# Layer two's stream in a new order: memory attention first, six state updates behind the output projection

## The chip, the core and the metric

The kernel runs on one core of one Trainium2 chip. The metric is the device time of one execution in microseconds. The engines are named as in the profile: PE multiplies matrices (PEld is its loading of weights), DVE and ACT work on vectors, POOL and SP are used here almost only to issue transfers. Each engine executes its own instructions in a fixed order; semaphores make it wait for others.

## The reference, cut to what matters

One step of a two-layer decoder trunk, for 256 prompt tokens and 8 sample tokens at once (264 columns in all), width 2048. Layer one mixes tokens by sliding-window attention, layer two by a gated linear recurrence; both have four memory cross-attention heads beside it. The change is in layer two:

```python
q, f, iv, mq, g = split(h @ w_in)             # one projection of 2048 to 12*128 (q, f, v), 512 (mq), 2048 (g)
fg = lb + (1 - lb) * sigmoid(f)               # 12 heads of 128; k = 1 - fg
# prompt: chunked recurrence per head; sample: one step from a given state (8 tokens x 12 heads x 128x128)
state = fg[..., None] * state + k[..., None] * v        # hgrn_state_sample, an output
o = einsum('bhk,bhkv->bhv', silu(q), state)
o = o * rsqrt(mean(o * o) + eps) * norm_w
mem_o = softmax(mq @ mk.T * 128 ** -0.5) @ mv           # 4 heads, 256 memory rows; caches for the sample tokens
branch = concat([o, mem_o]) * silu(g)
h = layer_norm(alpha * h + branch @ w_out)
```

## The kernel before

Tokens lie in the free axis: an activation is 128 features x 264 columns, sixteen such chunks make the width. A weight tile of 2048 x 128 (1 MB) is one *unit* of a stream (`Stream`). SP loads it into `raw` (four buffers); `prep` splits it into two halves of 16 bits, the high one on ACT (L97), the low one on DVE (L98), into `hl` (four buffers); then the unit's function runs `proj`: 16 chunks times three matmuls (high-high, low-high, high-low) of 128x264 into a PSUM bank `pj`, of which there are two. What becomes of the bank depends on the unit: `f_unit` makes gate and key (`fg`, `qk32`, `kk`), `hv_unit` copies values (`hvt` with one buffer, `vs`), to be transposed on PE as `hvp` and `hvr`, `hq_unit` makes the query `hqs`, gate units make silu (`sil`), `out_unit` adds to the residual `xres`.

Work that isn't a projection stands in generators beside the stream; after each unit `pump` takes one step of the first. `hg_side` is the recurrence of a pair of heads, ten steps: products level by level (`hd`, `hs_1` to `hs_64`, in two banks `sc`), then `pk` (transposed keys, copied to `kn`), `pu` (the chunk's state, copied to `s`), `hpo` (output, copied to `osb`), squares into `osq`, `rms` (their sum over features), and on ACT `Ln` and `Exp` for the root, each behind a table load; the last DVE operation (L1189) writes `mix` for the gate. `memp_side` and the `ck` and `cv` units are memory attention for prompt and sample tokens.

`state_unit` runs per head: it loads a state of 512 KB as a unit, multiplies it by the query (`hos`), and updates it in place, block by block for eight tokens: a matmul `vb` that spreads a value row, a scaling on ACT (L1237) and a multiply-add on DVE (L1238), and writes it out on POOL's queue (`out_ss`).

Layer two's order in the stream is by pairs: f, f, v, v, then q, state and (for heads 0 to 7) gate of each head; then four memory queries; then eight cache tiles, with the late gates dealt between them; then sixteen output tiles. A tile scheduler decides, from the order in which the code issues and its own estimates, the order of instructions on each engine; it is fixed when the program is built.

Of the kernel before, what the change touches and what calls it, by code (L numbers as in the profile page):

```python
# [18 lines left out]
P = 128  # L19
NC = 16  # L20
# [13 lines left out]
NG1 = 8  # L34
# [12 lines left out]
LEVELS = (1, 2, 4, 8, 16, 32, 64)  # L47
NMASK = (len(LEVELS) - 1) * 64
# [9 lines left out]
class Stream:  # L58


    def __init__(self, nc, pool, nraw, nsplit):
        self.nc, self.pool = nc, pool
        self.nraw, self.nsplit = nraw, nsplit
        self.units = []
        self.raw = {}
        self.hl = {}

# [37 lines left out]
    def run(self, pump):  # L105
        n = len(self.units)
        loaded = prepped = 0
        free = 0

        def loads():  # L110
            nonlocal loaded
            while loaded < n and loaded < free + self.nraw:
                self.load(loaded)
                loaded += 1

        loads()
        for i in range(n):
            while prepped < min(loaded, i + self.nsplit):
                self.prep(prepped)
                if self.units[prepped][5] and free == prepped:  # L120
                    free += 1
                prepped += 1
                loads()
            self.units[i][1](self.hl.pop(i))
            del self.raw[i]
            while free < prepped and (free <= i or self.units[free][5]):
# [8 lines left out]
def trunk_kernel(  # L135
# [75 lines left out]
    bias_s = pm.tile([P, 2, NQ], F32, name="bias_s")  # L211

# [503 lines left out]

    fin = {0: deque(), 1: deque()}
# [14 lines left out]
    def silu2(out, pt):  # L732
        nc.scalar.activation(out, pt, AF.Tanh, scale=0.5 * CP)
        nc.vector.scalar_tensor_tensor(out, out, 1.0, pt, op0=ALU.add, op1=ALU.mult)
# [10 lines left out]
    def residual(l, i, cols, n, pt):  # L745
        z = xres[:, i, cols]
        summed = nc.vector.scalar_tensor_tensor(z, z, ALPHA / CP, pt, op0=ALU.mult, op1=ALU.add)  # L747
# [235 lines left out]
    def f_unit(h):  # L983
        def fn(hl):
# [6 lines left out]
            if i == 0:  # L991
                cur["fg"] = p1.tile([P, 2, T], F32, tag="fg", name=f"fg{h}", bufs=2)
                cur["qk"] = p1.tile([P, 2, 2, TP], F32, tag="qk32", name=f"qk32_{h}", bufs=2)
                cur["kk"] = p1.tile([P, 2, TS], F32, tag="kk", name=f"kk{h}", bufs=2)
                cur["ks8"] = p1.tile([P, 2, TS], F32, tag="ks8", name=f"ks8{h}", bufs=2)
            fg, kk, ks8 = cur["fg"][:, i], cur["kk"][:, i], cur["ks8"][:, i]
# [6 lines left out]
            nc.vector.tensor_scalar_mul(ks8, kk, 1.0 / (SA * SK))  # L1003
# [5 lines left out]
    def hq_unit(h):  # L1009
        def fn(hl):  # L1010
# [5 lines left out]
            if h % 2 == 1:  # L1016
                side.append(hg_side(h // 2, cur["q"], cur["vn"], cur["fg"], cur["qk"]))
# [3 lines left out]
    later, due = [], []  # L1021

    def hv_unit(h):
        def fn(hl):
# [3 lines left out]
            if i == 0:  # L1028
                cur["vn"] = p1.tile([P, 2, 2, P], F32, tag="vn", name=f"vn{h}", bufs=2)
                cur["vr"] = p1.tile([P, 2, P], F16, tag="vr", name=f"vr{h}", bufs=2)  # L1030
# [10 lines left out]
    def hv_rows(h, vt, vs, vn, vr):  # L1041
# [7 lines left out]
        nc.vector.tensor_copy(vr[:, i], p16)  # L1049
# [14 lines left out]
    def hg_side(pi, q, vn, fg, qk):  # L1064
# [119 lines left out]
        for i, sq in enumerate(sqs):  # L1184
# [3 lines left out]
            scaled = mix[:, h] if h >= NG1 else sq  # L1188
# [3 lines left out]
            if h < NG1:  # L1192
# [4 lines left out]
    def state_unit(h):  # L1197
        def fn(hl):
            p1 = H["p"]
            pi, i = h // 2, h % 2  # L1200
            raw = stream.raw[state_at[h]][:, : TS * P]
            R = raw.rearrange("p (b v) -> p b v", b=TS)
            v = hl[:, :, : TS * P].rearrange("p s (b v) -> p s b v", b=TS)
            vr, fgs, ks8 = cur["vr"][:, i], cur["fg"][:, i, TP:T], cur["ks8"][:, i]
            qs, vts = (cur[n][:, i, TP:T] for n in ("q", "vt"))
            ks = cur["kk"][:, i]
            if i == 0:
                osb[pi] = p1.tile([P, 2, T], F32, tag="osb", name=f"osb{pi}", bufs=2)
            qk = p1.tile([P, TS], F32, tag="qk", name=f"qk{h}", bufs=2)
            qf = p1.tile([P, TS], F32, tag="qf", name=f"qf{h}", bufs=2)  # L1210
            qfh = p1.tile([P, TS, 2], F16, tag="qfh", name=f"qfh{h}", bufs=2)
            nc.vector.scalar_tensor_tensor(qf, qs, SA * 0.5 * CP, fgs, op0=ALU.mult, op1=ALU.mult)
            nc.vector.scalar_tensor_tensor(qk, qs, 8.0 * 0.5 * CP / SK, ks, op0=ALU.mult, op1=ALU.mult)
            qkh = p1.tile([P, 2, TS], F16, tag="qkh", name=f"qkh{h}", bufs=2)
            nc.scalar.activation(qkh[:, 0], qk, AF.Copy)
            nc.vector.tensor_tensor(qkh[:, 1], qk, qkh[:, 0], op=ALU.subtract)
            nc.scalar.activation(qfh[:, :, 0], qf, AF.Copy)
            nc.vector.tensor_tensor(qfh[:, :, 1], qf, qfh[:, :, 0], op=ALU.subtract)
            po = bank("ms", 1, f"hos{h}")
            pov = po[:, : 2 * TS].rearrange("p (b s) -> p b s", s=2)  # L1220
            for b in range(TS):
                mm(pov[:, b], v[:, 0, b], qfh[:, b], start=True, stop=False)
                mm(pov[:, b, 0:1], v[:, 1, b], qfh[:, b, 0:1], start=False, stop=True)
            pq = po[:, 2 * TS : 3 * TS]
            for s in range(2):
                mm(pq, H["ones"], qkh[:, s], start=s == 0, stop=s == 1)
            nc.vector.tensor_reduce(qf, pov, axis=AX.X, op=ALU.add)
            nc.vector.tensor_tensor(qk, pq, vts, op=ALU.mult)
            nc.vector.scalar_tensor_tensor(osb[pi][:, i, TP:T], qf, 1.0 / (SA * SA), qk, op0=ALU.mult, op1=ALU.add)
            for g in range(2):  # L1230
                pvb = bank("pt", 2, f"vb{h}{g}")
                for bb in range(4):
                    mm(pvb[:, bb * P : (bb + 1) * P], H["sel"][:, 4 * g + bb], vr, start=True, stop=True)
                for bb in range(4):
                    b = 4 * g + bb
                    s = R[:, b]
                    nc.scalar.activation(s, s, AF.Copy, scale=fgs[:, b : b + 1])  # L1237
                    nc.vector.scalar_tensor_tensor(  # L1238
                        s, pvb[:, bb * P : (bb + 1) * P], ks8[:, b : b + 1], s, op0=ALU.mult, op1=ALU.add
                    )  # L1240
            nc.gpsimd.dma_start(ss_o[pi, :, i * TS * P : (i + 1) * TS * P], raw)
# [3 lines left out]
    state_at = {}  # L1245
    for pi in range(HD // 2):
        for part, unit in (("f", f_unit), ("v", hv_unit)):
            for i in range(2):
                stream.add(wb(w_in1, NB1[part] + 2 * pi + i), unit(2 * pi + i))
        for h in (2 * pi, 2 * pi + 1):  # L1250
            stream.add(wb(w_in1, NB1["q"] + h), hq_unit(h))
            state_at[h] = len(stream.units)
            stream.add(state[pi][:, (h % 2) * TS * P : (h % 2 + 1) * TS * P], state_unit(h), SA, whole=True)
            if h < NG1:
                stream.add(wb(w_in1, NB1["g"] + h), early_gate(h))
    for h in range(NM):
        stream.add(wb(w_in1, NB1["mq"] + h), mq_unit(h))
# [4 lines left out]
    u = stream.units[-1]  # L1262
    stream.units[-1] = (u[0], mem1_sides(u[1]), *u[2:])

    def g1(j):
        stream.add(wb(w_in1, NB1["g"] + j), gate_unit(1, j))

    late = deque(range(NG1, NC))
    for n, (c, unit, t) in enumerate([(c_mk, ck_unit, t) for t in range(4)] + [(c_mv, cv_unit, t) for t in range(4)]):
        stream.add(c[1, t], unit(1, t), SA)  # L1270
        if late and (late[0] < NQ or n == 7 or late[0] < NQ + 2 and n > 3):
            g1(late.popleft())
    while late:
        g1(late.popleft())
    for i in range(NC):
        stream.add(wb(w_o[1], i), out_unit(1, i), home=hold if i >= NC - NSPLIT else None)

    def after(i):
# [8 lines left out]
        pump(1)  # L1287
# [23 lines left out]
def _constants():  # L1311
# [17 lines left out]
    for b in range(TS):  # L1329
        sel[b, b] = 1  # L1330
        sel[TS + b, b] = 1
# [101 lines left out]
```

## Time and profile before

| | |
|---|---|
| time, median of 3 runs | 906.81 us (906.51 to 907.01) |
| profiled execution | 906.08 us, its span 904.3 us |
| mean granted clock of TensorE | 0.994 of full |
| PE, DVE, ACT, POOL busy | 98%, 78%, 64%, 4% |
| read and written in HBM | 180 MB and 17 MB, 218 GB/s |

Layer two begins at about 430 us of the span; the last pair's chain and the memory attention are at 760 to 800, the output projection from there to about 880. Busy times are sums over an engine; the windows that the prediction shows give them for a stretch, with the granted clock (PEclk) beside.

### The profile page before, as it was taken

To read this page: it belongs to the slowest core of one execution; us is meant where nothing else is said; L and a number is where in the kernel's file an instruction comes from. 1 tells how busy PE (TensorE), PEld (TensorE's weight loads), DVE (VectorE), ACT (ScalarE), POOL (GpSimd) and SP (SyncE) were. 2 spreads that over 40 slices of the span, in tenths; PEclk is the share of its full clock that TensorE was granted. 3 is DMA by queue.
4 is the path that set the end of the run, shared out by engine and by line. 5 is a ranking of instruction groups with operands and counts; after the bars stand their busy time and mean duration, and the time that the engine had idled before them with its cause. 6 is when DMAs were issued, how large, how long until landed. Compare 5 with 4: busy or idle time off the path is not lost.

```text
span 904.3 us, 21814 instructions
## 1 busy us (share of the span) xinstructions
PE 886.6 (98%) x9281; PEld 762.9 (84%) x9281; DVE 701.5 (78%) x1230; ACT 582.4 (64%) x982; POOL 34.9 (4%) x68
## 2 busy tenths in 40 slices
PE   9999999999999999999999999999999999799996
PEld 6888889678888888876888888898888888688996
DVE  6879877669886666697687887979788989678736
ACT  6767776657664444476766877777777585858415
POOL 1100010000000000002000000000000000000000
PEclk9999999999999999999999999999999999899999
DMA  9998566557785555556374655827454878456303
GB/s 340 392 353 317 188 245 209 188 208 265 262 333 192 187 192 203 207 198 214 127 292 137 216 201 174 299 101 260 160 215 164 303 283 308 172 207 244 130 2 97
DMA packets 37853, 198.67 MB, mean 220 GB/s; under 512 B 4555, under 2 KB 10732, under 8 KB 17532
## 3 DMA queue, kind: packets, MB, share of 16 engines
q1 hardware_dynamic: 33024, 181.55, 56.3%
q0 software_dynamic: 4688, 15.67, 4.6%
q8 instruction: 72, 1.18, 0.5%
q14 instruction: 25, 0.20, 0.1%
q10 hardware_dynamic: 44, 0.07, 0.0%
HBM read 180.03 MB, written 17.22 MB: 218 GB/s over the span
## 4 chain that ended last, share of the span: by engine, by line
PE 77%; DVE 8%; ACT 6%; DMA 6%; issue 3%; SPq 0%; ACTq 0%; DVEq 0%
PE o L303 5%; PE o L305 5%; PE o L304 5%; PE g L305 5%; PE g L303 5%; PE g L304 5%; DVE hl L98 4%; ACT hl L97 2%; PE hv L305 2%; PE hv L303 2%; PE hv L304 2%; DMA raw<-in_w_in 2%; PE hq L303 2%; PE hq L305 2%; PE hq L304 2%
## 5 line engine op out<-in xcount | busy, mean ns | idle before, releaser
L98 DVE SCALAR_TENSOR_TENSOR hl<-raw,hl 128x2048 f16<-128x2048 f32 (+2 forms) x168 | 358.6, 2138 | 82.0 <-ACT hl L97 81.0
L97 ACT ACTIVATE hl<-raw 128x2048 f16<-128x2048 f32 (+2 forms) x168 | 299.2, 1784 | 97.8 <-PE o L305 45.4
L305 PEld LDWEIGHTS <-hl 128*128 128x128 f16 (+2 forms) x2048 | 197.4, 98 | 31.8 <-DVE hl L98 2.9
L303 PEld LDWEIGHTS <-hl 128*128 128x128 f16 (+2 forms) x2048 | 197.3, 98 | 30.6 <-issue 2.2
L304 PEld LDWEIGHTS <-hl 128*128 128x128 f16 (+2 forms) x2048 | 197.4, 98 | 30.3 <-issue 2.2
L305 PE MATMUL g<-xhl,hl 128*128 128x264 f16 x512 | 142.0, 277 | 2.4 <-DVE hl L98 2.4
L303 PE MATMUL g<-xhl,hl 128*128 128x264 f16 x512 | 141.9, 277 | 0.0
L304 PE MATMUL g<-xhl,hl 128*128 128x264 f16 x512 | 141.9, 277 | 0.0
L303 PE MATMUL o<-mix,hl 128*128 128x264 f16 x384 | 105.4, 276 | 0.8 <-DVE xres L747 0.8
L304 PE MATMUL o<-mix,hl 128*128 128x264 f16 x384 | 105.8, 276 | 0.0
L305 PE MATMUL o<-mix,hl 128*128 128x264 f16 x384 | 105.7, 276 | 0.0
L303 PE MATMUL q<-xhl,hl 128*128 128x264 f16 x192 | 53.0, 276 | 1.0 <-DVE kst L251 1.0
L303 PE MATMUL f<-xhl,hl 128*128 128x264 f16 x192 | 52.9, 276 | 0.4 <-DVE mvhl L251 0.4
L305 PE MATMUL hv<-xhl,hl 128*128 128x264 f16 x192 | 53.0, 276 | 0.0
L303 PE MATMUL hq<-xhl,hl 128*128 128x264 f16 x192 | 53.0, 276 | 0.0
L304 PE MATMUL hq<-xhl,hl 128*128 128x264 f16 x192 | 53.0, 276 | 0.0
L305 PE MATMUL hq<-xhl,hl 128*128 128x264 f16 x192 | 53.0, 276 | 0.0
L304 PE MATMUL hv<-xhl,hl 128*128 128x264 f16 x192 | 53.0, 276 | 0.0
L303 PE MATMUL hv<-xhl,hl 128*128 128x264 f16 x192 | 53.0, 276 | 0.0
L304 PE MATMUL q<-xhl,hl 128*128 128x264 f16 x192 | 53.0, 276 | 0.0
L305 PE MATMUL q<-xhl,hl 128*128 128x264 f16 x192 | 53.0, 276 | 0.0
L304 PE MATMUL f<-xhl,hl 128*128 128x264 f16 x192 | 52.9, 276 | 0.0
(338 smaller groups left out, 1858.4 us busy)
## 6 DMA issues: line engine op xcount, KB each, us to landing
raw<-in_w_in SPq DMA_DIRECT2D x88, 1024.0 KB, 6.4
raw<-in_w_o SPq DMA_DIRECT2D x32, 1024.0 KB, 5.0
raw<-in_w_mk SPq DMA_DIRECT2D x8, 1024.0 KB, 4.9
raw<-in_w_mv SPq DMA_DIRECT2D x8, 1024.0 KB, 4.9
raw<-in_c_mk SPq DMA_DIRECT2D x8, 1024.0 KB, 5.1
raw<-in_c_mv SPq DMA_DIRECT2D x8, 1024.0 KB, 7.0
raw<-in_state SPq DMA_DIRECT2D x12, 512.0 KB, 5.4
out_ss<-raw POOLq DMA_DIRECT2D x12, 512.0 KB, 5.5
```

The lines of the kernel that those rows point to most:

```text
L97: hi = self.nc.scalar.activation(hl[:, 0, s], raw[:, s], AF.Copy, scale=scale)
L98: lo = self.nc.vector.scalar_tensor_tensor(hl[:, 1, s], raw[:, s], scale, hl[:, 0, s], op0=ALU.mult, op1=ALU.subtract)
L303: mm(out, lhs(0), rhs(0), start=start, stop=False)
L304: mm(out, lhs(0), rhs(1), start=False, stop=False)
L305: return mm(out, lhs(1), rhs(0), start=False, stop=stop)
```

## The change

Layer two's stream is put together anew. Memory queries and cache tiles come first, dealt between the first pair's f, v, q and the gates of heads 0 and 1. A table `pumps` says how many pair steps follow each unit (0, 1 or 2). States are loaded per pair as one tile of 1 MB, and `state_unit` works per pair. Heads 0, 1, 2, 4, 6 have an early gate (a gate unit that stands ahead of the head's result); the others' gates follow the last pair, heads 10 and 11 at the end.

For heads 6 to 11 the update of the state is put off. Their value rows, gates and keys are copied (`kept`, 80 KB a pair) to HBM by POOL's queue and read back into `late_kept`; the state is fetched a second time, into the memory of `mkhl`, `mvhl` and `mqhl`, which memory attention no longer needs; and the update is issued in output units 1, 3, 5, 7, 9 and 11, on DVE behind the residual of that tile. `issue_after` binds instructions to the one named only on the engine that issued it, which here is DVE.

```diff
-NG1 = 8
+EARLY = (0, 1, 2, 4, 6)
+LATER = tuple(range(6, HD))
...
-            scaled = mix[:, h] if h >= NG1 else sq
+            scaled = sq if h in EARLY else mix[:, h]
...
+    def update(h, R, vr, fgs, ks, sel):
+        for g in range(2):
+            pvb = bank("pt", 2, f"vb{h}{g}")
+            for bb in range(4):
+                mm(pvb[:, bb * P : (bb + 1) * P], sel[:, 4 * g + bb], vr, start=True, stop=True)
+            for bb in range(4):
+                b = 4 * g + bb
+                s = R[:, b]
+                nc.scalar.activation(s, s, AF.Copy, scale=fgs[:, b : b + 1])
+                nc.vector.scalar_tensor_tensor(
+                    s, pvb[:, bb * P : (bb + 1) * P], ks[:, b : b + 1], s, op0=ALU.mult, op1=ALU.add
+                )
+        nc.gpsimd.dma_start(ss_o[h // 2, :, h % 2 * TS * P : (h % 2 + 1) * TS * P], R.rearrange("p b v -> p (b v)"))
...
+    def fetch(h):
+        if not homes:
+            aside["sel"] = cp.tile([P, TS, P], F16, tag="ms", name="late_sel", bufs=2)
+            nc.gpsimd.dma_start(aside["sel"], sel_d)
+            aside["kept"] = cp.tile([P, len(LATER), KEPT], F32, tag="ms", name="late_kept", bufs=2)
+            for pi in sorted(kept):
+                k = 2 * pi - LATER[0]
+                nc.gpsimd.dma_start(aside["kept"][:, k : k + 2], kept[pi])
...
+        nc.gpsimd.dma_start(aside[h], state[h // 2][:, (h % 2) * TS * P : (h % 2 + 1) * TS * P])
...
+    def with_update(fn, k):
+        def f(hl):
+            fn(hl)
+            with tc.issue_after(marks["o"].ins):
+                late_update(LATER[k])
+                if k + 3 < len(LATER):
+                    fetch(LATER[k + 3])
...
+            if 2 * pi in LATER:
+                tail = vr[:, :, P // 2 :]
+                nc.vector.tensor_copy(tail[:, :, :TS], fgs)
+                nc.vector.tensor_copy(tail[:, :, TS:], ks)
+                nc.gpsimd.dma_start(kept[pi], vr)
+                return
...
+    f_of(0)
+    for h in range(NM):
+        w1("mq", h, mem1_sides(mq_unit(h)) if h == NM - 1 else mq_unit(h))
+    cache(c_mk, ck_unit, 0)
+    f_of(1, 2)
+    cache(c_mk, ck_unit, 1)
+    v_of(0, 2)
...
+    for pi in range(2, HD // 2):
+        gated = 2 * pi - 2 in EARLY
+        f_of(2 * pi, 2)
+        f_of(2 * pi + 1, 1 if gated else 2)
+        v_of(2 * pi, 2)
+        v_of(2 * pi + 1, 2)
+        q_of(2 * pi)
+        q_of(2 * pi + 1)
+        state_of(pi)
+        if 2 * pi in EARLY:
+            gate_of(2 * pi)
+    last = (HD - 2, HD - 1)
...
+    for k, j in enumerate([j for j in range(NC) if j not in EARLY and j not in last] + list(last)):
+        w1("g", j, fetch_first(gate_unit(1, j)) if k == 6 else gate_unit(1, j))
     for i in range(NC):
-        stream.add(wb(w_o[1], i), out_unit(1, i), home=hold if i >= NC - NSPLIT else None)
+        unit = out_unit(1, i)
+        if i % 2 == 1 and i // 2 < len(LATER):
+            unit = with_update(unit, i // 2)
+        stream.add(wb(w_o[1], i), unit, home=hold if i >= NC - NSPLIT else None)
...
-        pump(1)
+        pump(pumps.get(i, 1))
```

The first place is the chain of pair 3 (heads 6 and 7) on PE. In the kernel before, the matmuls of that chain stand between those of the projections `hq`:

```order
L1152 MATMUL pk_9001<-ident,qk_6_7952 128x128 x4
...
L305 MATMUL hq_9018<-xhl,hl_8779 128x264
L1158 MATMUL pu_9070<-vn_8108,kn_9006 128x128 x4
L1169 MATMUL hpo_9155<-st_8506,vn_8108 128x128
L1170 MATMUL hpo_9155<-st_8506,vn_8108 128x128
L1045 MATMUL hvp_9081<-ident,hvt_8897 128x128 x2
...
L304 MATMUL hq_9170<-xhl,hl_8932 128x264
L1171 MATMUL hpo_9155<-qk_6_7952,s_9075 128x128
L1169 MATMUL hpo_9155<-st_8506,vn_8108 128x128
L1048 LDWEIGHTS vs_5660
L1048 MATMUL hvr_9085<-ident_68,vs_5660 128x128
L1170 MATMUL hpo_9155<-st_8506,vn_8108 128x128
```

Between the rows shown are 24 and 10 projection matmuls from `pk` to `pu`, and 29 from `pu` to the second `hpo`. In the changed kernel the same chain stands on PE like this, between the projections `hv` of head 11 and `hq` of head 10:

```order
L1156 MATMUL pk_9303<-ident,qk_6_8440 128x128 x4
L1173 MATMUL hpo_9378<-st_8877,vn_8599 128x128
L1174 MATMUL hpo_9378<-st_8877,vn_8599 128x128
L1162 MATMUL pu_9367<-vn_8599,kn_9308 128x128 x4
L1049 MATMUL hvp_9390<-ident,hvt_9254 128x128 x2
L1175 MATMUL hpo_9378<-qk_6_8440,s_9372 128x128
L1173 MATMUL hpo_9378<-st_8877,vn_8599 128x128
L1174 MATMUL hpo_9378<-st_8877,vn_8599 128x128
L1175 MATMUL hpo_9378<-qk_6_8440,s_9372 128x128
L1052 LDWEIGHTS vs_5662
L1052 MATMUL hvr_9394<-ident_68,vs_5662 128x128
L1049 MATMUL hvp_9467<-ident,hvt_9254 128x128 x2
```

Two rows on, `hvr` of the other head and the first matmul of `hq` follow: no projection matmul is left between the steps.

The second place is ACT in the same stretch of the changed kernel. `hvt` and `vs` are head 10's and 11's, `osq` are pair 3's squares, then `Ln` (L1187) and `Exp` (L1190); L1209 are the eight scalings of the put-off state of head 8, which the code issues in output unit 5:

```order
L1038 ACTIVATE hvt_9851<-hv_9800 128x264
L253 ACTIVATE vs_5662<-hv_9800 128x8
L1038 ACTIVATE hvt_9851<-hv_9912 128x264
L1181 ACTIVATE osq_9386<-osb_8899 128x264
L1181 ACTIVATE osq_9388<-osb_8899 128x264
L253 ACTIVATE vs_5663<-hv_9912 128x8
L1209 ACTIVATE mqhl<-mqhl,late_kept 128x128 x8
L1187 ACT_TABLE_LOAD
L1187 ACTIVATE osq_9386<-rms_9454,eps_rms 128x264
L1187 ACTIVATE osq_9388<-rms_9457,eps_rms 128x264
L1190 ACT_TABLE_LOAD
L1190 ACTIVATE osq_9386<-osq_9386 128x264
```

In the kernel before, the scalings (there L1237) of a head stand in its own state unit; head 8's have moved here, between squares and `Ln` of pair 3, and those of heads 6 and 7 stand in the same way around the `Ln` of pair 2.

The third place is the chain of the last pair (heads 10 and 11) on PE. Before, it stands behind a late gate and ahead of the sample tokens' memory attention (`mrow`, `mback`, `mso`):

```order
L1152 MATMUL pk_10521<-ident,qk_10_9379 128x128 x4
L1169 MATMUL hpo_10636<-st_10088,vn_9535 128x128
L1170 MATMUL hpo_10636<-st_10088,vn_9535 128x128
L1158 MATMUL pu_10565<-vn_9535,kn_10526 128x128 x4
L666 MATMUL mrow_10687<-ident,mst_10685 32x128 x2
L1171 MATMUL hpo_10636<-qk_10_9379,s_10570 128x128
L1169 MATMUL hpo_10636<-st_10088,vn_9535 128x128
L1170 MATMUL hpo_10636<-st_10088,vn_9535 128x128
L1171 MATMUL hpo_10636<-qk_10_9379,s_10570 128x128
L677 MATMUL mback_10698<-ident,mrows_10690 128x32 x2
L1182 MATMUL rms_10704<-osq_10644,ones_rms 128x264
L1182 MATMUL rms_10707<-osq_10646,ones_rms 128x264
```

In the changed kernel it stands ahead of the rest of the first two output tiles (`o`), and the put-off `vb` matmuls of head 6 stand between its steps:

```order
L1156 MATMUL pk_10667<-ident,qk_10_9659 128x128 x4
L1173 MATMUL hpo_10814<-st_10124,vn_9849 128x128
L1174 MATMUL hpo_10814<-st_10124,vn_9849 128x128
L1162 MATMUL pu_10743<-vn_9849,kn_10672 128x128 x4
L1205 LDWEIGHTS late_sel
L1205 MATMUL vb_11141<-late_kept,late_sel 128x128
...
L1175 MATMUL hpo_10814<-qk_10_9659,s_10748 128x128
L1173 MATMUL hpo_10814<-st_10124,vn_9849 128x128
L1174 MATMUL hpo_10814<-st_10124,vn_9849 128x128
L1175 MATMUL hpo_10814<-qk_10_9659,s_10748 128x128
...
L1186 MATMUL rms_10886<-osq_10822,ones_rms 128x264
...
L307 MATMUL o_0_11029<-mix,hl_10826 128x264
```

Memory attention is gone from there; the output projection's first tiles follow the chain's `rms`, with the low halves and the last chunks of `mix` still to come.

More of the change, by code (lines that the diff above doesn't have):

```diff
@@ L125, in run @@
             del self.raw[i]
-            while free < prepped and (free <= i or self.units[free][5]):
+            while free < prepped and (free + self.longer.get(free, 0) <= i or self.units[free][5]):
                 free += 1
@@ L211, in trunk_kernel @@
     bias_s = pm.tile([P, 2, NQ], F32, name="bias_s")
+    kept = {pi: dp.tile([P, 2, KEPT], F32, name=f"kept{pi}") for pi in sorted({h // 2 for h in LATER})}
     def small_work():
@@ L1198, in fn @@
         def fn(hl):
             p1 = H["p"]
[L1200 to L1208, printed above, removed]
@@ L1215, in fn @@
[L1215 to L1223, printed above, removed]
@@ L1224, in fn @@
-            pq = po[:, 2 * TS : 3 * TS]
+            qkh = p1.tile([P, 2, 2, TS], F16, tag="qkh", name=f"qkh{pi}", bufs=2)
+            split_from(qfh[:, :, :, 0], qfh[:, :, :, 1], qf, 1.0)
+            split_from(qkh[:, 0], qkh[:, 1], qk, 1.0)
+            po = bank("ms", 1, f"hos{pi}")
+            pov = po[:, : 4 * TS].rearrange("p (i b s) -> p i b s", i=2, s=2)
+            for i in range(2):
+                for b in range(TS):
+                    mm(pov[:, i, b], v[:, 0, i, b], qfh[:, i, b], start=True, stop=False)
+                    mm(pov[:, i, b, 0:1], v[:, 1, i, b], qfh[:, i, b, 0:1], start=False, stop=True)
@@ L1225, in fn @@
+            pq = po[:, 4 * TS : 6 * TS]
             for s in range(2):
-                mm(pq, H["ones"], qkh[:, s], start=s == 0, stop=s == 1)
+                mm(pq, H["ones"], qkh[:, s].rearrange("p i b -> p (i b)"), start=s == 0, stop=s == 1)
             nc.vector.tensor_reduce(qf, pov, axis=AX.X, op=ALU.add)
[L1228 to L1240, printed above, removed]
@@ L1241, in fn @@
-            nc.gpsimd.dma_start(ss_o[pi, :, i * TS * P : (i + 1) * TS * P], raw)
-        return fn
[L1245 to L1255, printed above, removed]
@@ new lines, in fn, with half, w1, state_of @@
+            R = raw.rearrange("p (i b v) -> p i b v", i=2, b=TS)
+            def half(i):
+                update(2 * pi + i, R[:, i], vr[:, i, : P // 2].bitcast(F16), fgs[:, i], ks[:, i], H["sel"])
+            half(0)
+            later.append(lambda: half(1))
+        return fn
+    state_at, pumps = {}, {}
+    def w1(part, i, fn, n=1):
+        pumps[len(stream.units)] = n
+        stream.add(wb(w_in1, NB1[part] + i), fn)
+    def state_of(pi):
+        at = state_at[pi] = len(stream.units)
+        pumps[at] = 0
+        whole = 2 * pi not in LATER
+        if whole:
+            stream.longer[at] = 1
+        stream.add(state[pi], state_unit(pi), SA, whole=whole)
@@ L1259, in mem1_sides, with gate_of, cache @@
+    def gate_of(h, n=1):
+        w1("g", h, early_gate(h) if h in EARLY else gate_unit(1, h), n)
+    def cache(c, unit, t):
+        pumps[len(stream.units)] = 0
+        stream.add(c[1, t], unit(1, t), SA)
     def mem1_sides(fn):
         return with_side(fn, [lambda h=h: memp_side(1, h) for h in range(NM)])
[L1262 to L1274, printed above, removed]
+    def f_of(h, n=1):
+        w1("f", h, f_unit(h), n)
+    def v_of(h, n=1):
+        w1("v", h, hv_unit(h), n)
+    def q_of(h, n=1):
+        w1("q", h, hq_unit(h), n)
+    f_of(0)
@@ new lines, in trunk_kernel, with fetch_first, f @@
+    v_of(3, 2)
+    q_of(2)
+    q_of(3)
+    state_of(1)
+    gate_of(2)
+    for pi in range(2, HD // 2):
[10 more added lines that the diff above has]
+    last = (HD - 2, HD - 1)
+    def fetch_first(fn):
+        def f(hl):
+            fn(hl)
+            with tc.issue_after(marks["silu"].ins):
+                for h in LATER[:3]:
+                    fetch(h)
+        return f
@@ L1329, in _constants @@
     for b in range(TS):
[L1330 to L1331 removed]
+        sel[b, b] = 1 / (SA * SK)
+        sel[TS + b, b] = 1 / (SA * SK)
     c["sel"] = sel
```

66 lines of the change are left out of this document (50 added, 16 removed).

## The prediction

> **What bounds the kernel now.** I read the page's first part, then layer two in stretches of 20 us and, where PE falls short, of 5 us.
>
> ```profile
> span 904.3 us, 21814 instructions
> PE 886.6 (98%) x9281; PEld 762.9 (84%) x9281; DVE 701.5 (78%) x1230; ACT 582.4 (64%) x982; POOL 34.9 (4%) x68
> ```
> ```profile
> core 0: us, PE busy (x) PEld busy (x) DVE busy (x) ACT busy (x) POOL busy (x), PEclk, DMA share, GB/s
> 740.00:760.00 20.00, 20.00 (x248) 17.69 (x247) 20.00 (x23) 14.40 (x14) 0.00 (x0) 1.00 0.91 327
> 760.00:780.00 20.00, 16.23 (x184) 13.44 (x182) 13.03 (x20) 11.82 (x19) 0.54 (x1) 0.95 0.66 240
> 780.00:800.00 20.00, 18.27 (x211) 15.25 (x210) 19.67 (x34) 15.73 (x30) 0.00 (x0) 0.88 0.58 220
> 800.00:820.00 20.00, 19.70 (x176) 17.12 (x175) 12.37 (x19) 12.12 (x18) 0.00 (x0) 1.00 0.30 103
> 820.00:840.00 20.00, 20.00 (x180) 17.39 (x178) 17.94 (x19) 14.23 (x11) 0.00 (x0) 1.00 0.92 339
> 840.00:860.00 20.00, 19.52 (x231) 18.49 (x230) 14.78 (x22) 7.83 (x9) 0.00 (x0) 1.00 0.20 79
> ```
>
> PE is the bound: 98% of the span. Layer two loses time almost only at 760 to 800, where the last head pair's chain meets the memory attention: 3.77+1.73 = 5.5 us idle, and a granted clock of 0.95 and 0.88, worth (0.05+0.12) x 20 = 3.4 us. The rows 800 and 840 add 0.30+0.48 = 0.8. So 9.7 us is what a perfect layer two would win. Busy time hides a little more, since matmuls follow each other faster than one lasts (0.11 against 0.28 us, first rows below), 0.17 us in each gap; with a dozen gaps 12 us is the most. I take 10.5.
>
> What an uncovered pair chain looks like is in the timeline of that stretch:
>
> ```profile
> 767.16 0.28 PE L305 MATMUL g<-xhl,hl 128*128 128x264 f16 x1
> 767.27 0.28 PE L303 MATMUL g<-xhl,hl 128*128 128x264 f16 x1
> ...
> 769.24 1.91 ACT L97 ACTIVATE hl<-raw 128x2048 f16<-128x2048 f32 x1 [3.84 <-issue]
> 769.31 0.63 PE L1152 MATMUL pk<-ident,qk 128*128 128x128 f32 x4
> 771.06 0.36 ACT L1147 ACTIVATE st<-hs 64x256 f32<-64x256 f32 x1
> 771.32 0.58 ACT L1154 ACTIVATE kn<-pk 128x512 f32<-128x512 f32 x1
> 772.02 1.09 PE L1158 MATMUL pu<-vn,kn 128*128 128x128 f32 x8
> 773.15 0.38 ACT L1162 ACTIVATE s<-pu 128x256 f32<-128x256 f32 x1 [1.25 <-PE pu L1158]
> 774.93 0.57 ACT L1173 ACTIVATE osb<-hpo 128x512 f32<-128x512 f32 x1
> 775.53 0.73 ACT L1177 ACTIVATE osq<-osb 128x264 f32<-128x264 f32 x2
> 776.41 1.28 ACT L1183 ACT_TABLE_LOAD   x1
> 777.71 0.85 ACT L1183 ACTIVATE osq<-rms,eps_rms 128x264 f32<-128x264 f32 x2
> 778.58 1.28 ACT L1186 ACT_TABLE_LOAD   x1
> 779.87 0.73 ACT L1186 ACTIVATE osq<-osq 128x264 f32<-128x264 f32 x2
> ...
> 780.33 0.90 DVE L1189 SCALAR_TENSOR_TENSOR mix<-osb,small_t,osq 128x264 f32<-128x264 f32 x2 [3.67 <-ACT osq L1186]
> ```
> ```profile
> 770.00:775.00 5.00, 3.02 (x22) 2.53 (x22) 3.19 (x5) 2.81 (x7) 0.40 (x1) 1.00 0.39 120
> 775.00:780.00 5.00, 3.90 (x54) 3.08 (x55) 0.72 (x3) 4.91 (x10) 0.15 (x1) 0.81 0.56 220
> 780.00:785.00 5.00, 3.71 (x95) 3.10 (x93) 4.67 (x8) 5.00 (x7) 0.00 (x0) 0.84 0.01 3
> 785.00:790.00 5.00, 4.57 (x28) 3.46 (x29) 5.00 (x7) 5.00 (x9) 0.00 (x0) 0.66 0.67 236
> 790.00:795.00 5.00, 5.00 (x46) 4.25 (x45) 5.00 (x11) 2.09 (x6) 0.00 (x0) 1.00 0.98 400
> ```
>
> In program order `pk`, `hpo`, `pu`, `hpo`, `rms` of this pair stand one behind the other on PE; the other pairs of before mostly have 10 to 50 projection matmuls between them and loses next to nothing (row 740, PE 20.00 of 20). From the start of `pu` to the end of `mix` the chain takes 781.23-772.02 = 9.2 us, and after it the granted clock is down: (0.19+0.16+0.34) x 5 = 3.4 us over three rows.
>
> **The change, part by part.** PE loses 12 `pq` matmuls of eight columns, DVE the `ks8` products and half of the state unit's eight-column operations; DVE is busy 78%, so that lies beside PE and is worth nothing. POOL's queue gets three writes and three reads of the kept rows, a second load of `sel` and six state loads, at 4% busy; only the reads have someone waiting (place A and B). SP's queue is moved past fewer, larger loads: a state tile now waits for the write of an older one, three to four projection units (16 us or more) ahead of use, against 12 us for the write and the load (6 each, rows below); hidden, and 0 to 2 us if the units run short.
>
> *Memory attention first.* Before's junction goes, as does what little stands around it: -10.5 (-9.7 to -12). The stages that now open layer two are projections interleaved with memory steps, and PE has two units of 48 matmuls between a step and its use; I take 0, and 0 to 2 for its bound.
>
> What is late next is read from where PE has nothing to do in the new order. There are three such places. They are priced with these groups and queues of layer two, and with a row of its timeline in which eight state scalings stand together:
>
> ```profile
> 691.86 2.45 ACT L1237 ACTIVATE raw<-raw,fg 128x128 f32<-128x128 f32 x8 [0.50 <-DVE hl L98]
> ```
> ```profile
> L1001 ACT ACTIVATE qk<-th,hl_lb 128x256 f32<-128x256 f32 x4 | 2.4, 588 | 0.0
> L1046 ACT ACTIVATE vn<-hvp 128x256 f32<-128x256 f32 x6 | 2.3, 376 | 0.0
> L1034 ACT ACTIVATE hvt<-hv 128x264 f32<-128x264 f32 x4 | 1.5, 384 | 3.5 <-PE hv L305 3.5
> L249 ACT ACTIVATE vs<-hv 128x8 f16<-128x8 f32 x4 | 0.7, 168 | 0.0
> L728 DVE SCALAR_TENSOR_TENSOR sil<-sil,mix 128x264 f32<-128x264 f32 x8 | 3.4, 430 | 2.0 <-ACT mix L634 1.9
> L729 ACT ACTIVATE mix<-sil 128x264 f16<-128x264 f32 x8 | 3.4, 420 | 4.7 <-DVE sil L728 4.7
> L1238 DVE SCALAR_TENSOR_TENSOR raw<-vb,ks,raw 128x128 f32<-128x128 f32 x48 | 13.4, 345 | 0.0
> ```
> ```profile
> out_ss<-raw POOLq DMA_DIRECT2D x6, 512.0 KB, 6.1
> raw<-in_state SPq DMA_DIRECT2D x4, 512.0 KB, 6.2
> ...
> out_sp<-s POOLq DMA_DIRECT2D x6, 128.0 KB, 3.1
> ```
>
> *Place A, pair 2's chain between `hv9` and `hq8`.* `hq8` takes the PSUM bank of `hv8`, so its first matmul waits until `hvt` and `vs` of head 8 are copied. `hvt` has one buffer and is free only after `hvp` of head 7, which the new order puts behind all of `hv9` and pair 2's `hpo`. From there ACT has the rest of a weight split, `osb` 0.57, two `qk32` of 0.588, `vn` 0.376, `hvt` 0.384, `vs` 0.168, and DVE one more `vs` (0.16): 2.8 us and up to 1.9 for the split, less some 0.6 of `hvr` and `hvp` on PE: 2.2 to 4.1, I take 3.4. Then eight scalings of head 6's put-off state (L1209, was L1237; 2.45) stand on ACT between the squares and `Ln`, six of head 7's between the two `Ln`s (1.8) and two behind (0.6), and they wait for `late_kept`, which was written to HBM and is read back: 2 x 3.1 = 6.2 us by the 128 KB row, of which I put 3 behind the moment at which ACT arrives (0 to 6.2). From the squares to the tanh of `hq8` ACT then needs 0.7+2.45+1.3+0.4+1.8+0.4+0.6+1.3+0.4+0.4 = 9.8 us plus that wait, 12.8; PE has `hq8` and `hq9`, 96 matmuls of 0.112 = 10.8, and 0.7 of small ones until `f10` needs the bank: 11.5. So 1.3 shows (0 to 4.5, for a whole round trip). Place A: 4.7 (2.2 to 8.6).
>
> *Place B, pair 3's chain between `hv11` and `hq10`.* Here all of the chain stands between two projections: `st` 0.36, `kn` 0.58, `pu` 1.09, `s` 0.38, `hpo` 0.6, `osb` 0.57, two `qk32` 1.18, `vn` 0.38, `hvt` 0.38, `vs` 0.17+0.16: 5.9 us, in which PE has 1.3 of its own: 4.6 (3.5, if the `qk32` go first, to 5.9). Then the same scalings for head 8, waiting for their own round trip, stand between the squares and `Ln`. `hd` and `hs` of pair 4 wait for that `Ln` (they take its PSUM banks): squares, scalings, table load and `Ln` 0.7+2.45+1.3+0.85 = 5.3, against 5.4 of `hq10` as cover, so nothing, or 3 with the same 3 us of the round trip; half-way 1.5 (0 to 4.5). Place B: 6.1.
>
> *Place C, pair 5's chain between the last gates and the output projection.* `hs_64`, `pk`, `hpo`, `pu`, `hpo`, `rms` are adjacent again, as in before's junction, and memory attention is no longer there to fill even a part. The third output tile needs a third bank and the first two need the last `mix`. `st`+`kn` 0.9, 9.2 from `pu` to `mix`, then gate, cast and low half 0.43+0.42+0.43: 11.4, less 4.1 of PE's own (`pk` 0.6, `pu` 1.1, `hpo`, `rms` and eight `vb` an estimated 2.4): 7.3 (6.5 to 8).
>
> *Clock.* Before's rows show the clock falling behind 5 us windows in which PE did 3.0 to 3.9 of work as recorded; it cost 3.4 there. I take 3 for all three places (0 to 6). The Trainium skill (TensorE: Matmul & The Clock Gate, "Part 1: The HAM clock gate") says that one idle window of about 3.4 us puts TensorE at half rate until about 3.4 us were busy; the 0.81, 0.84 and 0.66 agree with it. By that rule each place would pay 3.4 x 0.5 = 1.7 us for each window that falls idle, 5 in all.
>
> *Updates put off.* Six heads' 8 DVE updates, 8 scalings and 8 `vb` matmuls move behind the output tiles 1, 3, 5, 7, 9, 11. Before, DVE is at 17.94 of 20 in 820:840; six updates of 8 x 0.345 = 2.8 us push it over what a 5.4 us unit leaves, and the fetch of head 9 comes only after head 6's write (6.1+6.2 us on POOL's queue), with ACT waiting in order. PE has weights in hand for two units: 1 (0 to 3). The tail after 860 is unchanged.
>
> Sum: -10.5+4.7+6.1+7.3+3+1 = +11.6; span 915.9. The profiled execution was 906.08, 1.8 beside its span, and 0.7 below the median of 906.81: **918.4 us**. Its own range is 909 to 929: the small ends together give a span of 904.3-12+2.2+3.5+6.5+0+0 = 904.5, the great ones 904.3-9.7+8.6+10.4+8+6+3 = 930.6; neither comes whole. A measurement tells about 0.2% (1.8 us) from no change.
>
> **The rivals.** *The places are filled (faster, 0.2).* If ACT and DVE run so far ahead of PE that `hvt`, `st` and `kn` are done when PE arrives, A and B cost nothing and only C is left, partly (3): 904.3-10.5+3 = 896.8, and 2.5 beside the span: 899 us, 896 to 904. For it: ACT and DVE are busy 64% and 78%. Against: every wait in A and B starts from a PE result of the same chain, which no early start of another engine shortens. It decides when A, B and C together are below 10.5.
>
> *Only the chains cost, the round trips are hidden (slower or the same, 0.17; of it 0.07 within 0.2%).* The kept rows land before ACT arrives: A 3.4, B 4.6, C 6.5 and a clock of 1.5 give 904.3-10.5+16 = 909.8, a time of 912.3; with chains a third shorter, 907. For it: ACT may come to the scalings later than I think, behind its own queue of splits.
>
> *The clock falls at all three and stays (0.08).* Gaps in a row, as in A and B where two waits are 5 us apart, keep the clock down over whole projection units: a unit of 48 matmuls in 10.8 in place of 5.4 us. Two such units more: 918.4+10.8 = 929 us. Against it: before's fall was over by 790, at 1.00 again.
>
> That leaves 0.55 for the sum. Range for 8 in 10: 899 (half of the first rival below it) to 931.
>
> **What would show it.** The memory attention's own stage at the start of layer two with PE at 20.00 of 20; three dips of PE in the second half: waits `PE hq <- DVE vs` of 3 to 5 us, twice, with ACT L1209 beside it waiting for the DMA of `late_kept`; and before the output projection one of 7 us behind `mix` with two table loads on ACT. The prediction is wrong if PE shows no `hq` wait over 1 us, or if the output projection, not the gates' end, loses most.

## The result, and the profile after

The changed kernel took **928.1 us** (median of 4 runs, 925.5 to 929.3), against 906.9 before: ratio 1.023, 95% interval 1.0208 to 1.0252. The forecast was 918.4, in a range of 899 to 931: slower, as it said, by nearly twice as much (21.2 us for 11.6). The profiled execution took 929.3, its span is 927.5.

The page and the windows of 20 us of the changed kernel where PE falls short:

```profile
span 927.5 us, 21725 instructions
PE 892.9 (96%) x9269; PEld 763.6 (82%) x9269; DVE 694.3 (75%) x1176; ACT 581.2 (63%) x964; POOL 42.1 (5%) x81
```
```profile
520.00:540.00 20.00, 18.86 (x192) 15.93 (x191) 15.92 (x18) 16.79 (x33) 0.00 (x0) 1.00 0.56 207
540.00:560.00 20.00, 19.83 (x224) 17.82 (x222) 18.35 (x39) 12.15 (x20) 1.08 (x2) 1.00 0.73 261
...
660.00:680.00 20.00, 16.79 (x135) 13.96 (x133) 5.62 (x17) 12.16 (x32) 1.64 (x3) 0.91 0.35 120
680.00:700.00 20.00, 18.29 (x223) 15.59 (x220) 17.86 (x28) 15.69 (x23) 0.00 (x0) 1.00 0.41 140
700.00:720.00 20.00, 16.47 (x162) 13.96 (x161) 15.40 (x30) 12.02 (x22) 1.08 (x2) 0.98 0.67 240
720.00:740.00 20.00, 17.60 (x165) 14.33 (x163) 9.94 (x18) 13.09 (x24) 0.54 (x1) 0.94 0.17 57
...
800.00:820.00 20.00, 17.88 (x176) 15.19 (x175) 10.25 (x15) 9.65 (x15) 0.54 (x1) 1.00 0.45 161
820.00:840.00 20.00, 16.17 (x125) 13.17 (x125) 12.49 (x22) 11.47 (x14) 0.54 (x1) 0.83 0.23 76
840.00:860.00 20.00, 18.15 (x170) 15.77 (x168) 16.09 (x22) 14.10 (x16) 1.61 (x3) 1.00 0.95 355
860.00:880.00 20.00, 17.24 (x205) 16.26 (x205) 19.93 (x44) 12.07 (x24) 2.13 (x4) 1.00 0.48 177
```

Before's dip at 760 to 800 is gone, and four others are there: place A at 660 to 700 (4.9 us idle, and 0.09 x 20 = 1.8 of clock), B at 700 to 740 (5.9 and 1.6), C at 800 to 840 (6.0 and 3.4), and the output projection at 840 to 880 (4.6). What PE waited for in layer two of the changed kernel (line, releaser: total, times, longest), and ACT's waits at A, B and C from its timeline:

```profile
PE hq L307 <- DVE vs L255: 4.8, 2, 2.9
PE o L307 <- ACT mix L734: 4.8, 1, 4.8
PE o L307 <- DVE xres L752: 4.6, 3, 2.6
PE hs L307 <- ACT qk L1083: 3.7, 6, 1.1
```
```profile
673.43 2.45 ACT L1209 ACTIVATE mkhl<-mkhl,late_kept 128x128 f32<-128x128 f32 x8 [4.38 <-DMA late_kept<-kept]
...
722.36 2.44 ACT L1209 ACTIVATE mqhl<-mqhl,late_kept 128x128 f32<-128x128 f32 x8 [3.73 <-DMA late_kept<-kept]
...
818.17 1.28 ACT L1187 ACT_TABLE_LOAD   x1
...
820.33 1.28 ACT L1190 ACT_TABLE_LOAD   x1
...
823.35 0.77 ACT L734 ACTIVATE mix<-sil 128x264 f16<-128x264 f32 x2 [0.99 <-DVE sil L733]
```

All three places are there as read from the order: `hq` behind `vs` twice, ACT 4.4 and 3.7 us in the wait for the read-back with a pair's `Ln` behind it, and the output projection behind the last `mix`, 4.8 us at the end alone.

A tile's row gives the first and the last start of a matmul: `hd` is a pair chain's first, `rms` its last. Before (L1120, L1182) and changed (L1124, L1186):

```profile
L1120 PE MATMUL hd<-hqs,qk x48: 272/275/275, 459.3 to 731.3; 128*128 128x128 f32 x48
L1182 PE MATMUL rms<-osq,ones_rms x24: 386/386/490, 506.9 to 776.8; 128*128 128x264 f32 x24
```
```profile
L1124 PE MATMUL hd<-hqs,qk x48: 272/275/377, 490.5 to 777.7; 128*128 128x128 f32 x48
L1186 PE MATMUL rms<-osq,ones_rms x24: 386/386/647, 560.2 to 818.7; 128*128 128x264 f32 x24
```

The six chains run one behind the other (`st` and `prod` have one buffer). The first begins 31 us later than before, because memory attention now stands ahead of the first query, and takes 69.7 us in place of 47.6, while memory attention's splits, softmax and tiles share ACT and DVE with it; that this sharing is the reason is borne out by the runs below that move memory attention beside other chains. The last ends 42 us later.

### The profile page after: what moved, and what is told of

It reads as the page before. It is cut to its first block, busy times and chain, and to the rows that moved or that the text cites. A ratio compares the mean times of both kernels' runs of the same rounds, so it can differ in the third digit from the quotient of the medians.

```text
span 927.5 us, 21725 instructions
## 1 busy us (share of the span) xinstructions
PE 892.9 (96%) x9269; PEld 763.6 (82%) x9269; DVE 694.3 (75%) x1176; ACT 581.2 (63%) x964; POOL 42.1 (5%) x81
## 4 chain that ended last, share of the span: by engine, by line
PE 61%; issue 24%; DVE 5%; DMA 5%; ACT 4%; POOL 1%; SPq 0%; ACTq 0%; POOLq 0%; DVEq 0%
PE g L307 5%; PE g L308 5%; PE g L309 5%; PE o L307 5%; PE o L309 5%; PE o L308 5%; PE q L307 2%; PE q L309 2%; PE q L308 2%; DVE hl L101 2%; PE mq L308 2%; PE mq L307 2%; PE mq L309 2%; PE mk L307 2%; PE mk L308 2%
## 5 line engine op out<-in xcount | busy, mean ns | idle before, releaser
L307 PE MATMUL o<-mix,hl 128*128 128x264 f16 x384 | 106.8, 279 | 7.4 <-ACT mix L734 4.8
L308 PE MATMUL o<-mix,hl 128*128 128x264 f16 x384 | 106.8, 278 | 0.0
L309 PE MATMUL o<-mix,hl 128*128 128x264 f16 x384 | 106.8, 278 | 0.0
L307 PE MATMUL hq<-xhl,hl 128*128 128x264 f16 x192 | 54.3, 283 | 4.9 <-DVE vs L255 4.8
L309 PE MATMUL hq<-xhl,hl 128*128 128x264 f16 x192 | 54.2, 282 | 0.0
L308 PE MATMUL hq<-xhl,hl 128*128 128x264 f16 x192 | 54.1, 282 | 0.0
## 6 DMA issues: line engine op xcount, KB each, us to landing
l_d<-l_t POOLq DMA_DIRECT2D x4, 861.0 KB, 12.9
```

The source lines that it names most:

```text
L307: mm(out, lhs(0), rhs(0), start=start, stop=False)
L308: mm(out, lhs(0), rhs(1), start=False, stop=False)
L309: return mm(out, lhs(1), rhs(0), start=False, stop=stop)
```

## The experiments

Theory 1, from the prediction: the hoisted scalings (issued in the output units, but standing on ACT in the chains of pairs 2 and 3) and their read-back, and the adjacent chains, cost it. Theory 2, from the rows above: the end of the last chain sets the time. The ratios stand against the kernel before on the same chip.

**The scalings bound to their output tile** (e1_bound)

```diff
-        squared = nc.scalar.activation(sq[:, :n], z, AF.Square)
+        squared = marks["sq"] = nc.scalar.activation(sq[:, :n], z, AF.Square)
-            with tc.issue_after(marks["o"].ins):
+            with tc.issue_after(marks["o"].ins), tc.issue_after(marks["sq"].ins):
```

> The changed kernel with the put-off scalings on ACT queued behind the square of their own output tile as well, so that none can stand between another pair's squares and Ln. Theory 1 (hoisted scalings, and the read-back of the kept rows for which they wait, cost the second half of places A and B, and the delay moves the rest of the chains so that C has no filler): A keeps its first wait, about 3.5 us with the small ones, B and C get projection matmuls between their steps and lose 2 to 3 together, the output projection keeps its 5: 928 - 4 - 7 - 8 = about 909 us (905 to 915). Rival (the scalings only fill time in which ACT has nothing to do; what costs is the adjacent chains): within 4 us of 928, 924 to 930.

Measured: 909.5 us, ratio 1.0040 (1.0027 to 1.0053). In its windows:

```profile
660.00:680.00 20.00, 16.96 (x166) 14.83 (x166) 11.63 (x26) 13.54 (x24) 1.63 (x3) 1.00 0.31 117
680.00:700.00 20.00, 20.00 (x242) 17.68 (x240) 19.46 (x31) 14.50 (x19) 0.00 (x0) 1.00 0.64 233
700.00:720.00 20.00, 16.69 (x156) 14.03 (x154) 10.97 (x25) 12.36 (x24) 1.62 (x3) 1.00 0.42 152
720.00:740.00 20.00, 18.98 (x236) 16.27 (x235) 18.51 (x31) 12.23 (x16) 0.00 (x0) 1.00 0.35 117
...
800.00:820.00 20.00, 17.68 (x157) 15.12 (x157) 9.97 (x12) 14.49 (x24) 0.00 (x0) 1.00 0.28 95
...
840.00:860.00 20.00, 19.29 (x229) 18.22 (x227) 19.68 (x40) 13.75 (x30) 2.13 (x4) 1.00 0.60 230
```
```profile
L1186 PE MATMUL rms<-osq,ones_rms x24: 386/386/490, 558.4 to 805.0; 128*128 128x264 f32 x24
```

About 18 of the 21 us go with one binding: 21.2 us over the kernel before become 3.4. A keeps its first wait (3.0), B and C lose less (4.3 and 2.3), the output projection's 4.6 become 0.7, and the clock stays at 1.00. Pair 4's chain begins 12.9 us earlier (713.8 in place of 726.7) and the last one ends 13.7 us earlier; the two waits (4.4+3.7) and the 7.4 us of scalings that had stood in the chains of pairs 2 and 3 add up to 15.5. With the last chain that much earlier, projections stand between its steps on PE again.

Theory 1's time came true in part by luck: it had 2 to 3 us for B and C together, where 6.6 were lost, and 5 for the output projection, where 0.7 were; the two misses cancel. The run takes out the scalings and the wait for the read-back together, so it doesn't say how much is due to each.

**Two buffers for `hvt`** (e2_hvt2, on the changed kernel; e9_bound_hvt2, on e1_bound)

```diff
-                cur["vt"] = p1.tile([P, 2, T], F32, tag="vt", name=f"hvt{h}", bufs=1)
+                cur["vt"] = p1.tile([P, 2, T], F32, tag="vt", name=f"hvt{h}", bufs=2)
-        s1 = p1.tile([P, 2, P], F32, tag="s1", name=f"s1{pi}", bufs=2)
+        s1 = p1.tile([P, 2, P], F32, tag="s1", name=f"s1{pi}", bufs=1)
```

> The changed kernel with two buffers for hvt (and one for s1, to make room); the scalings stay early. Theory 1: the first wait of A and of B (3.1 and 2.0 us, hq behind vs) goes, the waits for the kept rows stay: 922 to 925 us. Rival (hq's wait is not for the hvt buffer but for ACT's queue itself): no change, 926 to 930.

> e1_bound with two buffers for hvt (one for s1). Theory 2: the first wait at A (3.1 in e1_bound) only moves to the next step of the same chain, as it did in e2_hvt2, and the program order has the last chain's steps adjacent again: 908 to 916 us. Rival (the buffer alone is the wait): 904 to 907.

Measured: 923.2 us (1.0186, 1.0164 to 1.0209) and 915.4 (1.0103, 1.0080 to 1.0126). One row of PE's waits in layer two of each (e2_hvt2's third and e9_bound_hvt2's first row):

```profile
PE rms L1186 <- ACT osq L1181: 3.9, 2, 3.0
```
```profile
PE rms L1186 <- ACT osq L1181: 6.9, 3, 3.0
```

`hq` no longer waits for `vs`; PE waits for the squares of the same chain instead, 3.9 us in place of 4.8 with the scalings early, 6.9 in place of 2.9 with them bound. So e2_hvt2's time lies where theory 1 had it, but the wait moved where theory 1 had it go. A buffer doesn't shorten a chain; it only changes the instruction at which PE meets its end. With the scalings early it gave 4 to 5 us all the same, with them bound it cost 6: the last `rms` starts 3.8 us later (808.8 for 805.0), the `o` matmuls between the last chain's steps are used up before it, and PE then waits 4.8 us for `mix`, with a clock of 0.83 at 800 to 820.

**One part alone in the new order: no update put off** (e4_inline)

```diff
-LATER = tuple(range(6, HD))
+LATER = ()
```

> Memory attention first and the pump table alone: no update is put off, all twelve are made in their state unit. Theory 1: A and B lose their second half (no kept rows to wait for), C stays adjacent (9 us), the output projection loses its 5: 928 - 4 - 4 - 5 = about 915 us (910 to 921). Rival (the new order is a gain and the put-off updates are all of the loss): 897 to 905.

Measured: 923.6 us (1.0185, 1.0168 to 1.0203). Theory 1 and its rival both missed. Without read-back A, B and C cost as much as in the changed kernel, with the updates' scalings and multiply-adds beside the chains, and the last chain ends latest of all; the output projection loses nothing, since no update stands there:

```profile
L1186 PE MATMUL rms<-osq,ones_rms x24: 386/386/807, 560.8 to 825.3; 128*128 128x264 f32 x24
```

So in this order the put-off is worth 14 us (923.6 to 909.5), and the hoist loses it all and about 4 more.

**The other part alone: the order of before** (e5_oldorder, updates put off; e8_old_inline, not; e10_pumps, e8_old_inline with other pair steps; e12_old_late, e10_pumps with the updates put off and bound). Pairs, memory attention behind them, eight early gates; states per pair in all four.

```diff
+    for pi in range(HD // 2):
+        f_of(2 * pi)
+        f_of(2 * pi + 1)
+        v_of(2 * pi)
+        v_of(2 * pi + 1)
+        q_of(2 * pi)               # e10, e12: q_of(2 * pi, 2)
+        ...
+        state_of(pi)
+        pumps[len(stream.units) - 1] = 2     # e10, e12: 1
```

> The put-off updates alone: the order of before (pairs, then memory attention among the late gates), eight early gates, states per pair as in the changed kernel. The homes of the fetched states come free only after memory attention, so no scaling can be hoisted into a pair's chain. Theory 1: before's junction stays (9.7), the output projection loses 5 as in the changed kernel, pairs nothing or one hq wait of 3: 909 to 916 us. Rival (the put-off updates are the loss wherever they stand): 922 us or more.

> The order of before with states per pair, and no update put off: e5_oldorder without its put-off updates. If the states per pair (one split of 1 MB, sixteen updates in a row) lengthen the chains in that order: 915 to 925 us. Rival (the put-off updates were e5_oldorder's loss): 905 to 909.

> e8_old_inline with one pair step behind a state unit and two behind the first q of a pair, so that the steps stand where they stood in the kernel before (pk behind the second v). If e8_old_inline's loss came from the table of steps (values transposed behind pu, hq waiting): 905 to 912 us, last chain ended at about 776 to 780. Rival (one state tile per pair, split and updated in one piece, lengthens the chains): 917 to 924, last chain ended at 787 or later.

> e10_pumps with the six updates put off and their scalings queued behind the square of their output tile: the put-off alone, in the order of before. If taking 48 scalings and 48 multiply-adds out of pairs 3 to 5 shortens their chains, as e1_bound against e4_inline says (804 against 824): last chain ended 5 to 10 us earlier than e10_pumps' 782, the output projection 1 to 5 slower: 906 to 912 us. Rival (in this order the chains of pairs 3 to 5 wait for something else, and the put-off is only the output projection's cost): 915 to 920.

Measured: 923.8 (1.0206, 1.0174 to 1.0238), 922.1 (1.0168, 1.0135 to 1.0201), 914.0 (1.0083, 1.0065 to 1.0101), 918.5 (1.0130, 1.0095 to 1.0164). e5_oldorder fell on the rival's side, and e8_old_inline shows that it was not for the rival's reason: without the put-off nearly all of the loss stays, and the two intervals overlap. e10_pumps missed its range (905 to 912) by 2 us and its rival's by 3; e12_old_late fell on the rival's side. Where two steps of a pair stand decides 8 us (e8_old_inline to e10_pumps): with `pk` one unit too early, no projection matmul stands on PE beside the second half of pair 3's chain, from the end of `hv` at 684.4 to `hq` at 691.5; in e10_pumps `hv` and `hq` run on between its steps. The window 680 to 700 of e8_old_inline and of e10_pumps:

```profile
680.00:700.00 20.00, 15.81 (x133) 13.07 (x131) 11.31 (x34) 15.13 (x37) 1.37 (x3) 0.83 0.26 100
```
```profile
680.00:700.00 20.00, 20.00 (x195) 17.77 (x193) 15.70 (x40) 17.77 (x40) 1.61 (x3) 1.00 0.43 150
```

What is left of e10_pumps' loss, 7.6 us, lies at the junction (760 to 800), where the last chain ends 6 us later than before (782.7) and PE waits 5.9 us for the chain's level products (`hs`), for which it waited nowhere before. The states per pair are the main difference that remains; no run changes them alone, so that they cost it is not shown. In this order the put-off gains nothing: e12_old_late's last chain ends at 783.4, and it is some 4 us slower. Why the put-off shortens the end in the new order and not in this one stays open.

**The first chain earlier** (e6_first; e7_first6 with six early gates), on e1_bound:

```diff
+    for part in (f_of, v_of):
+        part(0)
+        part(1)
+    q_of(0)
+    gate_of(0)
+    q_of(1)
+    gate_of(1)
+    for h in range(NM):
+        w1("mq", h, ...)
+    state_of(0)
+    cache(c_mk, ck_unit, 0)
+    f_of(2, 2)
...
```

> As e1_bound, and the first pair's f, v, q and gates ahead of the memory queries, the cache tiles dealt between pair 1's units, and eight early gates. Theory 2 (the six pair chains, one behind the other, are the path: 490 to 804 in e1_bound, each 40 to 68 us; what counts is when the first begins and how long each lasts): the first chain begins at about 460, the last ends at about 775 to 785, A and B lose nothing, C at most what is lacking of filler: 897 to 905 us. Rival (a chain is as long as the ACT and DVE work beside it makes it, so memory attention only lengthens other chains): 908 to 915.

> As e6_first with six early gates (0, 1, 2, 4, 5, 6), so that ten late gates stand between the last query and the output projection. Theory 2: the same end of the last chain within 10 us but two more units of filler for it: 896 to 904 us, up to 4 below e6_first. Rival: without those gates between the pairs the chains lag and pair 3's place loses 4 to 6 again: 2 to 6 above e6_first.

Measured: 926.6 (1.0226, 1.0202 to 1.0251) and 924.2 (1.0202, 1.0177 to 1.0227). Both are outside theory 2's range by some 20 us; e6_first is outside its rival's (908 to 915) by 12. Theory 2's numbers failed on one point of it: the length of a chain was taken as given, and the rival was right that it is not. e6_first's rows:

```profile
L1124 PE MATMUL hd<-hqs,qk x48: 272/275/402, 457.8 to 785.8; 128*128 128x128 f32 x48
L1186 PE MATMUL rms<-osq,ones_rms x24: 386/386/490, 531.1 to 819.6; 128*128 128x264 f32 x24
```

The first chain did begin at 457.8, but lasted 73 us, the second 67, with memory attention beside both. The two more late gates of e7_first6 gave 2.4 us; the two intervals overlap.

**Memory attention moved, nothing else** (e11_mid3, e11_mid2), on the kernel before, with its states per head and its updates in place:

```diff
     for pi in range(HD // 2):
+        if pi == 3:                # e11_mid2: 2; cache tiles dealt between the f and v units from here on
+            for h in range(NM):
+                u = mq_unit(h)
+                stream.add(wb(w_in1, NB1["mq"] + h), mem1_sides(u) if h == NM - 1 else u)
...
+    for j in range(NG1, NC):
+        stream.add(wb(w_in1, NB1["g"] + j), gate_unit(1, j))
```

> The kernel before (states per head, nothing put off, eight early gates), with only the memory attention moved: memory queries behind pair 2, cache tiles dealt between the projections of pairs 3 and 4, all eight late gates at the end. Theory 2 (the path is the six chains; what matters at the end is that projections are left beside the last one): last chain ended at about 770 to 790 as before, its place filled by late gates, 893 to 903 us. Rival (memory attention in the middle lengthens chain 2 or 3 by more than it saves, as it did chain 0 in the changed kernel): 907 to 915.

> As e11_mid3, with the memory queries behind pair 1 and the cache tiles beside pairs 2 and 3. Theory 2: 893 to 903 us, within 3 of e11_mid3. Rival: 907 to 915.

Measured: 918.3 (1.0122, 1.0101 to 1.0143) and 919.6 (1.0145, 1.0129 to 1.0161): the rival, and more. e11_mid3's last chain, and its longest waits of PE in layer two:

```profile
L1182 PE MATMUL rms<-osq,ones_rms x24: 385/387/467, 508.0 to 817.5; 128*128 128x264 f32 x24
```
```profile
PE hs L303 <- ACT qk L1079: 7.0, 4, 3.3
PE hs L304 <- DVE qk L1080: 3.1, 2, 2.7
```

Up to the first `rms` it is the kernel before (508.0 against 506.9); with memory attention in the middle the last one starts at 817.5 in place of 776.8. The chain beside which it now stands, pair 3's, takes 67.6 us from its first `hd` to its `rms` (645.8 to 713.4) in place of 46.4, and PE waits 10.1 us for level products (`hs`) that ACT and DVE make; there was no such wait before. So moving memory attention ahead of the last pairs, with all late gates at the end, costs 11 to 13 us by itself. In the kernel before a good part of it stands behind the last chain, and 760 to 800 lose 8.9 us in all.

No version was faster than the kernel before; e1_bound is 0.4% slower than it and 2% faster than the changed kernel. The end of the last chain (theory 2) orders most versions of the new order, but not those of the old one: e5_oldorder's last chain ends at 783.6 and it takes 923.8 us, e1_bound's ends at 805.0 and it takes 909.5.

## Why the prediction was right

The direction, the three places and the order of their sizes came out, and the time lies in the range. The sum was too small: it put the span at 915.9, and the profiled one is 927.5, 11.6 us more. The steps, by their own order:

- *Memory attention first, -10.5.* The old junction is gone, as said. The opening was taken at 0 (0 to 2): 520 to 560 lost 1.3, where the prediction's signs had PE at 20.00. That the move also delays and lengthens the chains isn't in the sum; the prediction priced what moved by PE's idle time at the places, which includes it.
- *Place A, 4.7.* Measured 4.9 idle and 1.8 of clock. First wait taken at 3.4, measured 2.9; the rest at 1.3, measured 1.9. The wait of ACT for the read-back taken at 3, measured 4.4.
- *Place B, 6.1.* Measured 5.9 and 1.6 of clock. First part taken at 4.6, measured 3.5, of which the wait of `hq` for `vs` is only 1.9 (the signs asked for 3 to 5, twice); the rest taken at 1.5, measured 2.4. ACT's wait for the read-back taken at 3, of which half was counted, measured 3.7.
- *Place C, 7.3.* Measured 6.0 and 3.4 of clock; the wait behind `mix` is 4.8, where the signs had 7.
- *Clock, 3 for all three.* Measured 1.8+1.6+3.4 = 6.8. This term was too small by half.
- *Updates put off, 1 (0 to 3).* Measured 4.6, outside its bounds. The argument was "PE has weights in hand for two units". That step failed, but not for want of weights: PE waited for none there. What it lacked was a free bank, since all 4.6 us are `o` behind `xres`, the residual on DVE that empties the bank. ACT waited for head 9's state, which took 8.4 us to land; its next splits came late, DVE waited 2.8 us for the first of them, and the residual stands behind the low halves of these splits in DVE's order (PE's longest wait, 2.6 us, ends with it):

```profile
850.87 2.45 ACT L1209 ACTIVATE mkhl<-mkhl,late_kept 128x128 f32<-128x128 f32 x8 [4.05 <-DMA mkhl<-in_state]
...
855.15 2.29 DVE L101 SCALAR_TENSOR_TENSOR held<-raw,held 128x2048 f16<-128x2048 f32 x1 [2.81 <-ACT held L100]
...
860.25 0.42 DVE L752 SCALAR_TENSOR_TENSOR xres<-xres,o 128x264 f32<-128x264 f32 x1
```
```profile
mkhl<-in_state POOLq DMA_DIRECT2D x1, 512.0 KB, 8.4
```

Idle time at the three places came to 16.8 against 18.1 foretold; less 1.3 here, the clock (+3.8), the output projection (+3.6) and the opening (+1.3) make 7.4 of the 11.6 us between the two spans; the rest is not accounted for here. That the idle time agrees so well is partly luck, since the parts are off both ways.

Wrong in the prediction's picture is the weight of the causes. It gave the hoisted scalings and their read-back 1.3+1.5 = 2.8 us of idle time; e1_bound, which takes them out of the chains, gains about 18. It gave the adjacent steps at C 7.3 as a price of their own; in e1_bound C loses 2.3, so most of C's price hung on how late the last chain comes. A, B and C are not three separate prices: e2_hvt2 and e9_bound_hvt2 move a wait without removing it, and e4_inline keeps the loss without the round trips. Of the rivals, "the round trips are hidden" came closest to being tested by e1_bound: 912.3 foretold for it, 909.5 measured where ACT doesn't meet them. A and B are near what that rival had (3.0 and 4.3 for 3.4 and 4.6); C and the clock are not (2.3 and 0 for 6.5 and 1.5).

## What to carry to other kernels

Where an order-only binding names one engine's instruction, look at every other engine of the moved work: here ACT's half of a put-off update stood about 20 units early, in front of a `Ln` on the path, and one more binding gave back about 18 of 21 us. In a stream with serial side chains read the first and last start of a chain's first and last step in each version before moving filler: a wait that moves from one instruction to the next is the chain's end, and neither a buffer nor an earlier start helps when what stands beside the chain makes it longer. Change the table that says which step follows which unit only together with its order on the engines; two steps shifted by one unit cost 8 us.

## What the runs showed of the hardware

The clock that was lost (20 us times what the granted clock lacks, per window) comes in amounts near multiples of 1.7 us: 1.8 at A, 1.6 at B, 3.4 at C and in before's junction. Whether a gap costs clock can't be told from its length here: the same wait of `hq` for `vs`, 2.9 us, left the clock at 1.00 in the window 660 to 680 of e1_bound and brought 0.91 in that of the changed kernel, and a wait of 3.0 us brought 0.91 in that of e9_bound_hvt2. The Trainium skill (TensorE: Matmul & The Clock Gate, "Part 1: The HAM clock gate") puts the window at about 3.4 us and the lower rate at half, so an estimated 1.7 for each idle window; the size of the steps agrees with it. What decides whether a gap shorter than that window counts, no run here shows.
